# Order of the products in the split-weight projections: second parts of the weights last

## The chip, the cores and the metric

One core of a Trainium2 chip runs the whole program in one launch. The metric is the device time in microseconds of one execution; smaller is better. The times below are medians of runs on the chip. One further execution was profiled, and all rows come from that one.

## The reference, cut to what matters

Two transformer blocks act on 256 tokens of width 1024, all in float32.

```
first_block:   h = modulate(rms_norm(x)), also for 256 context tokens
               p = h @ w_in                       # q, k, v of 8 gated-delta heads and 4 linear-attention heads, gates
               gated delta rule (2 directions) -> @ w_out_a ; gated linear attention (2 directions) -> @ w_out_b
               (gated sum) @ w_out ; x += g1 * y
               mixture of 32 experts, top 4 of 32 ; x += g2 * y ; rms_norm
second_block:  h @ w_in_2 -> dilated attention and latent attention (w_uq_2, w_ukv_2)
               concat(norms) @ w_o_2 ; x += rms_norm(y)
               h @ w_up_2 -> depthwise convolution -> gelu(g) * v -> @ w_down_2 ; x += rms_norm(y)
```

Every `@` outside the experts and the attention cores is a projection of the kind that the change touches.

## The kernel before, in words

**Split weights.** The projections hand TensorE operands of the type `float32r`, and to keep float32's precision each is made of three products. Each float32 operand is split (`split`, lines 48 to 50): ScalarE rounds it to a first part ("hi": tiles `whi`, `hh`, `yT0h`, `hi`), then VectorE subtracts that from the original and leaves the second part ("lo": `wlo`, `hl`, `yT0l`, `lo`). For v of the first two pairs of heads GpSimd does the subtraction. `mm3` (lines 75 to 78) adds hi·hi, hi·lo and lo·hi into one PSUM bank for one block of 128 rows of the contraction. A loop around it goes over the blocks, usually eight.

**Two forms.** Where the output is wanted by feature (`gates`, `gdn_pair`, `stat_proj`, the second block's q and k, its `w_up_2`), the weights are the stationary operand and 256 or 512 tokens move. `mm3`'s second product (line 77) then takes the activations' second part, its third (line 78) the weights'. Where it is wanted by token (`tok_proj`, `out_proj` in `merge`, `tok_mm`, `down`, `down_last`) the activations are stationary and the weights move; there line 77 takes the weights' second part and line 78 the activations'. In the profile's names (out<-moving,stationary) `pj<-hh,wlo` is line 78 of the first form and `pj<-wlo,hh` line 77 of the second.

**Buffers.** The first and the second parts of weights have two buffers each (tags `whi` and `wlo`), each 128 x 1024 elements. ScalarE can round a third piece only when the last product that reads the first piece's `whi` is done; VectorE needs the same of `wlo`. PSUM has two banks for each of the names `pj`, `g` and `sc`.

**Stages, in order of time.** `pre` and `gates`; `gdn` over four pairs of heads, where the projections of the next pair and "fill" work (`lat_act`, `mod_steps`, `gla_proj`) run beside the triangular solve (VectorE, lines 515 and 516, whose result goes through DRAM to the tile `AB`) and the scan of the current pair; `gla` over four heads, each with the projections of the next; `merge` with three output projections, each after `to_feat` has made its activations block by block (transpose on TensorE in line 988, hi on ScalarE in line 990, lo on VectorE in line 991); `moe` with 32 experts whose weights are not split; `post`, the second block.

**What sets the order.** The program text gives priorities. A planner of the tile framework writes each engine's queue at compile time: among the instructions whose operands it reckons to be ready it takes the earliest in the text. Each queue is then worked off in order on the chip, waiting on semaphores. So instructions of different stages stand between each other, transposes among products for instance. The SP queue issues most weight loads, the POOL queue those of `w_in`; a landing buffer `w` is free when both parts were taken from it.

Of the kernel before, what the change touches and what calls it, by code (L numbers as in the profile page):

```python
# [15 lines left out]
P = 128  # L16
# [55 lines left out]
        v.scalar_tensor_tensor(y, a, 1.5, y, op0=OP.add, op1=OP.mult)  # L72


def mm3(nc, out, ah, al, bh, bl, first, last, **kw):
    nc.tensor.matmul(out, ah, bh, start=first, stop=False, **kw)  # L76
    nc.tensor.matmul(out, ah, bl, start=False, stop=False, **kw)  # L77
    nc.tensor.matmul(out, al, bh, start=False, stop=last, **kw)  # L78


def rows_T(K, pool, psum, name, parts):
# [149 lines left out]
def gates(K, dbg=None):  # L231
# [28 lines left out]
    nc.scalar.dma_start(wg[:, :, 32:64], w3[:, :, 7200:7232])  # L260
    wgh, wgl = wsplit(K, wg, P)
    ps = psum.tile([P, 512], F32, name="pj", bufs=2)
    for k in range(8):
        mm3(nc, ps, wgh[:, k, :], wgl[:, k, :], K.hh[:, k, :], K.hl[:, k, :], k == 0, k == 7)
    K.gr = c.tile([64, 512], F32, name="gr")
    nc.scalar.activation(K.gr, ps[:64, :], AF.Copy)

# [123 lines left out]
def gdn_pair(K, pr):  # L391
# [14 lines left out]
    for hh in range(2):  # L406
        h = pr * 2 + hh
        H = Ctx()
        heads.append(H)
        H.h = h  # L410
        H.qT = gp.tile([P, 256], F32, name="qT", bufs=2)
        H.kT = gp.tile([P, 512], F32, name="kT", bufs=4)
        vT = gp.tile([P, 512], F32, name="vT", bufs=1)
        for j, (dst, n) in enumerate(((H.qT, 256), (H.kT, 512), (vT, 512))):

            hi, lo = wsplit(K, ws[hh * 3 + j], P, nc.gpsimd if pr < 2 and j == 2 else None)
            ps = psum.tile([P, 512], F32, name="pj", bufs=2)
            for k in range(8):
                mm3(nc, ps[:, :n], hi[:, k, :], lo[:, k, :], K.hh[:, k, :n], K.hl[:, k, :n], k == 0, k == 7)
            conv_silu(K, ps[:, :n], n, j * 8 + h, dst, nc.vector)  # L420

        pk = K.G()
        for t in range(4):
            nc.tensor.transpose(pk[:, t * P:(t + 1) * P], H.kT[:, t * P:(t + 1) * P], K.ident)
        H.kt = gp.tile([P, 4, P], F32, name="kt", bufs=4)
        nc.scalar.activation(H.kt, pk.rearrange("p (t n) -> p t n", t=4), AF.Copy)
        ns = gp.tile([P, 6], F32, name="ns", bufs=2)
        sq = gp.tile([P, 512], F32, name="th", bufs=2)
        for t in range(4):
            nc.scalar.activation(sq[:, t * P:(t + 1) * P], H.kt[:, t, :], AF.Square, accum_out=ns[:, t:t + 1])  # L430
        pn = K.G()
        sq = gp.tile([P, 512], F32, name="th", bufs=2)
        nc.scalar.activation(sq[:, :2 * P], H.qT, AF.Square)
        for t in range(2):
            nc.tensor.matmul(pn[:, t:t + 1], sq[:, t * P:(t + 1) * P], K.ones[:, 0:1], start=(t == 0), stop=(t == 1),
                             skip_group_check=True)
        nc.vector.tensor_copy(ns[:, 4:6], pn[:, 0:2])
        nq = gp.tile([P, 6], F32, name="nq", bufs=2)
        nc.vector.tensor_scalar(nq, ns, 4 * EPS, None, op0=OP.add)
        r = gp.tile([P, 6], F32, name="r", bufs=2)  # L440
        rsqrt(K, gp, r, nq, 6)

        r2 = gp.tile([P, 6], F32, name="r2", bufs=2)
        nc.vector.tensor_mul(r2, r, r)
        H.d = gp.tile([P, 2, 4], F32, name="d", bufs=4)
        bh = K.beta.rearrange("p d c h -> p d c h")[:, :, :, h]
        nc.vector.tensor_mul(H.d, bh, r2[:, None, 0:4].to_broadcast([P, 2, 4]))
        hn = gp.tile([P, 4], F32, name="hn", bufs=2)
        nc.vector.scalar_tensor_tensor(hn, nq[:, 0:4], 0.5, r[:, 0:4], op0=OP.mult, op1=OP.mult)
        nc.vector.tensor_scalar(K.aq[:, :, h], nq[:, 4:6], 128.0 * EPS, None, op0=OP.mult)  # L450

        pv = K.G()
        for t in range(4):
            nc.tensor.transpose(pv[:, t * P:(t + 1) * P], vT[:, t * P:(t + 1) * P], K.ident)
        H.vs = gp.tile([P, 4, P], F32, name="vs", bufs=4)
        for t in range(4):
            nc.scalar.activation(H.vs[:, t, :], pv[:, t * P:(t + 1) * P], AF.Copy, scale=hn[:, t:t + 1])
        H.dk = gp.tile([P, 2, 4], F32, name="dk", bufs=4)
        nc.vector.tensor_mul(H.dk, H.d, K.kds.rearrange("p (d t h) -> p d t h", d=2, t=4)[:, :, :, h])
# [289 lines left out]
def stat_proj(K, col, n, out):  # L749

    nc = K.nc
    w3 = K.I["w_in"].rearrange("o (k p) n -> p (o k) n", p=P)
    w = K.ring.tile([P, 8, P], F32, name="w")
    nc.gpsimd.dma_start(w, w3[:, :, col:col + P])
    hi, lo = wsplit(K, w, P)
    for k in range(8):
        mm3(nc, out, hi[:, k, :], lo[:, k, :], K.hh[:, k, :n], K.hl[:, k, :n], k == 0, k == 7)


def tok_proj(K, col, tiles, done):  # L760

    nc = K.nc
    w3 = K.I["w_in"].rearrange("o (k p) n -> p (o k) n", p=P)
    ws = []
    for k4 in range(2):
        w = K.ring.tile([P, 4, 256], F32, name="w")
        nc.gpsimd.dma_start(w, w3[:, k4 * 4:k4 * 4 + 4, col:col + 256])
        ws.append(w)
    pss = [K.psum.tile([P, 512], F32, name="pj", bufs=2) for _ in range(len(tiles) // 2)]
    for k4 in range(2):  # L770
        hi = K.wsp.tile([P, 4, 256], F32R, name="whi", bufs=2)
        lo = K.wsp.tile([P, 4, 256], F32R, name="wlo", bufs=2)
        split(K, ws[k4], hi, lo)
        for t in tiles:
            o = pss[t // 2][:, t % 2 * 256:t % 2 * 256 + 256]
            ts = slice(t * P, (t + 1) * P)
            for kk in range(4):
                k = k4 * 4 + kk
                first = k == 0 and t % 2 == 0
                last = k == 7 and t % 2 == 1  # L780
                mm3(nc, o, K.hh[:, k, ts], K.hl[:, k, ts], hi[:, kk, :], lo[:, kk, :], first, last, skip_group_check=True)
    for t in tiles:
        done(t, pss[t // 2][:, t % 2 * 256:t % 2 * 256 + 256])

# [146 lines left out]
def merge(K, rc, dbg=None):  # L931
# [14 lines left out]
    def out_proj(name, lhs_hi, lhs_lo, order, done):  # L946

        pss = {}
        for n, k4 in order:
# [20 lines left out]
            by_token = order is K_OUTER and (n, k4) == order[-1]  # L970
            for t in range(2) if by_token else ():
                done(t, 0, pss[0][t])
            for t, kk in itertools.product(range(2), range(4)) if by_token else ((t, kk) for kk in range(4) for t in range(2)):
                ts, k = slice(t * P, (t + 1) * P), k4 * 4 + kk
                mm3(nc, pss[n][t], lhs_hi[:, k, ts], lhs_lo[:, k, ts], *pairs[kk], k == 0, k == 7)
                if by_token and kk == 3:
                    done(t, n, pss[n][t])
            for t in range(2) if order is N_OUTER and k4 == 1 else ():
                done(t, n, pss[n][t])
# [556 lines left out]
def post(K, dbg=None):  # L1536
# [53 lines left out]
    def tok_mm(name, k_n, col, n, hi, lo, outs):  # L1590

        kk = 2048 // n
        for k0 in range(0, k_n, kk):
            kc = min(kk, k_n - k0)
            w, _ = post_load(K, name, k0, kc, col, n)
            k2 = 0
            while k2 < kc:
                s = min(1024 // n, kc - k2)
                h_, l_ = wpair(1024)
                split(K, w[:, k2 * n:(k2 + s) * n], h_[:, :s * n], l_[:, :s * n])  # L1600
                for i in range(s):
                    k = k0 + k2 + i
                    for t in range(2):
                        ts = slice(t * P, (t + 1) * P)
                        mm3(nc, outs[t], hi[:, k, ts], lo[:, k, ts], h_[:, i * n:(i + 1) * n], l_[:, i * n:(i + 1) * n],
                            k == 0, k == k_n - 1)
                k2 += s


# [70 lines left out]
    for j2 in range(4):  # L1680
        _, wv = post_load(K, "w_in_2", 0, 8, j2 * 256, 256)
        for jj in range(2):
# [2 lines left out]
            hv, lv = (a.rearrange("p (k n) -> p k n", n=P) for a in (h_, l_))  # L1685
            split(K, wv[:, :, jj * P:(jj + 1) * P], hv, lv)
            p = bank("pj")
            for k in range(8):
                mm3(nc, p[:, :256], hv[:, k, :], lv[:, k, :], hi[:, k, :], lo[:, k, :], k == 0, k == 7)
            nc.vector.tensor_mul(qk[:, j, :], p[:, :256], rrb)  # L1690
    va = ap.tile([P, 2, 512], F32, name="va")
    ps = [bank("pj") for _ in range(2)]
# [128 lines left out]
    def down(acc, name, k2, lhs_hi, lhs_lo):  # L1821

        pairs = down_w(name, k2, [wpair(1024) for _ in range(2)])
        for kk, t in ((0, 0), (0, 1), (1, 0), (1, 1)):
            h_, l_ = pairs[kk]
            ts = slice(t * P, (t + 1) * P)
            for n in range(2):
                ns = slice(n * 512, (n + 1) * 512)
                mm3(nc, acc[t][n], lhs_hi[:, kk, ts], lhs_lo[:, kk, ts], h_[:, ns], l_[:, ns], k2 + kk == 0, False)

    def down_last(acc, name, k2, lhs, pairs):

        pairs = down_w(name, k2, pairs[:2]) + down_w(name, k2 + 1, pairs[2:])
        for t in range(2):
            ts = slice(t * P, (t + 1) * P)
            for n in range(2):
                ns = slice(n * 512, (n + 1) * 512)
                for k, (h_, l_) in enumerate(pairs):
                    mm3(nc, acc[t][n], lhs[k][0][:, ts], lhs[k][1][:, ts], h_[:, ns], l_[:, ns], False, k == 3)

    def gained(acc, g, t):

# [62 lines left out]
    for c2 in range(11):  # L1905
        us = {}
        for gv in range(2):
# [3 lines left out]
            for cc in range(2):  # L1911
# [2 lines left out]
                hv, lv = (a.rearrange("p (k n) -> p k n", n=P) for a in (h_, l_))  # L1914
                split(K, wv[:, :, cc * P:(cc + 1) * P], hv, lv)
                p = bank(("pj", "g")[cc])
                for k in range(8):
                    mm3(nc, p[:, :256], hv[:, k, :], lv[:, k, :], hi[:, k, :], lo[:, k, :], k == 0, k == 7)
                u = fp.tile([P, 256], F32, name="u", bufs=8)
                nc.scalar.activation(u, p[:, :256], AF.Identity, scale=K.tap2[1][ct], bias=K.cb2[:, ct:ct + 1])  # L1920
                nc.vector.scalar_tensor_tensor(u[:, 1:], p[:, 0:255], K.tap2[0][ct], u[:, 1:], op0=OP.mult, op1=OP.add)
# [90 lines left out]
```

## Time and profile before

| | |
|---|---|
| median of 3 runs | 2082.15 us (2078.74 to 2091.74) |
| the profiled execution, its own time | 2083.65 us |
| its span, first to last instruction | 2081.9 us |
| mean granted TensorE clock | 0.954 of full speed |
| TensorE matmul / weight load busy | 91% / 56% of the span |
| VectorE / ScalarE / GpSimd busy | 46% / 31% / 9% |
| HBM | 273 GB/s over the span |

Matmul records overlap, since they are pipelined and their ends are modelled, so the busy share is no share of peak. "idle before <-releaser" is the time for which an engine stood before an instruction, and the work whose end let it go on. Start times are microseconds from the span's start.

### The profile page before, as it was taken

To read this page: it belongs to the slowest core of one execution; us is meant where nothing else is said; L and a number is where in the kernel's file an instruction comes from. 1 tells how busy PE (TensorE), PEld (TensorE's weight loads), DVE (VectorE), ACT (ScalarE), POOL (GpSimd) and SP (SyncE) were. 2 spreads that over 40 slices of the span, in tenths; PEclk is the share of its full clock that TensorE was granted. 3 is DMA by queue.
4 is the path that set the end of the run, shared out by engine and by line. 5 is a ranking of instruction groups with operands and counts; after the bars stand their busy time and mean duration, and the time that the engine had idled before them with its cause. 6 is when DMAs were issued, how large, how long until landed. Compare 5 with 4: busy or idle time off the path is not lost. (4 is left out here: it accounts for less than half of the span.)

```text
span 2081.9 us, 27700 instructions
## 1 busy us (share of the span) xinstructions
PE 1898.8 (91%) x10742; PEld 1159.6 (56%) x10743; DVE 965.6 (46%) x2245; ACT 652.5 (31%) x1369; POOL 184.0 (9%) x247
## 2 busy tenths in 40 slices
PE   4796989799998999999999999999999889989998
PEld 1664768687986763333333333333333228779997
DVE  2797785857464641212122221221211137676777
ACT  2553545467554420000000000000000004555554
POOL 1343122211112000000000000000000000000000
PEclk8798999899999989999999999999999988998999
DMA  7347654437544689999999999999999994433551
GB/s 261 77 122 206 183 169 116 112 103 206 169 151 151 254 325 417 417 414 418 417 416 418 418 416 417 418 416 417 418 418 416 417 345 139 140 102 121 183 182 41
DMA packets 191939, 569.60 MB, mean 274 GB/s; under 512 B 47919, under 2 KB 90776, under 8 KB 158650
## 3 DMA queue, kind: packets, MB, share of 16 engines
q1 hardware_dynamic: 160064, 507.19, 63.1%
q0 software_dynamic: 13392, 47.72, 7.4%
q10 hardware_dynamic: 18346, 12.86, 2.5%
q8 instruction: 86, 1.41, 0.3%
q14 instruction: 51, 0.42, 0.1%
HBM read 555.22 MB, written 12.50 MB: 273 GB/s over the span
## 5 line engine op out<-in xcount | busy, mean ns | idle before, releaser
L50 DVE TENSOR_TENSOR wlo<-w,whi 128x1024 fp32r<-128x1024 f32 (+1 forms) x185 | 223.9, 1211 | 132.6 <-ACT whi L49 129.8
L1308 PE MATMUL pg<-w,xT 128*64 128x512 f32 x1024 | 274.4, 605 | 3.5 <-DMA w<-in_w_gu_dram 3.4
L1308 PE MATMUL pl<-w,xT 128*64 128x512 f32 x1024 | 268.1, 593 | 0.0
L49 ACT ACTIVATE whi<-w 128x1024 fp32r<-128x1024 f32 (+1 forms) x189 | 197.3, 1047 | 217.8 <-PE pj L77 70.4
L1330 PE MATMUL po<-w,aT 128*64 128x512 f32 x1024 | 239.9, 608 | 7.1 <-DMA w<-in_w_down_dram 5.7
L1230 ACT ACTIVATE th<-ga 128x512 f32<-128x512 f32 x32 | 20.2, 632 | 613.8 <-DVE ga L1228 613.8
L1338 DVE TENSOR_TENSOR o<-po,g 64x512 f32<-64x512 f32 x64 | 44.1, 689 | 260.1 <-PE po L1330 259.4
L1308 PEld LDWEIGHTS pl<-w,xT 128*64 128x64 f32 x1024 | 75.2, 137 | 146.4 <-issue 146.4
L1330 PEld LDWEIGHTS po<-w,aT 128*64 128x64 f32 x1024 | 69.5, 139 | 141.7 <-issue 121.9
L1308 PEld LDWEIGHTS pg<-w,xT 128*64 128x64 f32 x1024 | 65.2, 136 | 139.4 <-issue 115.9
L1228 DVE TENSOR_SCALAR ga<-pg 128x512 f32<-128x512 f32 x32 | 22.1, 691 | 244.8 <-PE pg L1308 244.8
L77 PE MATMUL pj<-wlo,hh 128*128 128x256 f32 x384 | 116.2, 303 | 2.8 <-DVE wlo L50 2.8
L76 PE MATMUL pj<-whi,hh 128*128 128x256 f32 x384 | 115.2, 300 | 2.9 <-ACT whi L49 2.9
L78 PE MATMUL pj<-whi,hl 128*128 128x256 f32 x384 | 114.6, 299 | 0.0
L76 PE MATMUL pj<-hh,whi 128*128 128x512 f32 (+1 forms) x264 | 100.9, 384 | 12.6 <-ACT hh L49 9.1
L372 DVE SCALAR_TENSOR_TENSOR acc<-padl,taps,acc 128x256 f32<-128x256 f32 x192 | 104.3, 557 | 10.1 <-ACT acc L365 8.0
L78 PE MATMUL pj<-hh,wlo 128*128 128x512 f32 (+1 forms) x264 | 100.0, 380 | 5.9 <-DVE wlo L50 5.7
L77 PE MATMUL pj<-hl,whi 128*128 128x512 f32 (+1 forms) x264 | 100.9, 382 | 0.1
L1288 POOL CAST se<-sel 128x128 fp32r<-128x128 f32 x32 | 22.4, 702 | 828.4 <-PE pl L1292 828.4
L1267 PEld LDWEIGHTS tr<-S,h 128*128 128x128 f32 x480 | 57.9, 191 | 48.6 <-issue 34.9
L77 PEld LDWEIGHTS pj<-wlo,hh 128*128 128x128 f32 x384 | 78.0, 203 | 11.0 <-DVE wlo L50 4.2
L1360 PE MATMUL y<-o,PwT 128*128 128x512 f32 (+1 forms) x136 | 72.2, 641 | 13.0 <-DVE o L1338 10.2
(682 smaller groups left out, 3601.7 us busy)
## 6 DMA issues: line engine op xcount, KB each, us to landing
w<-in_w_gu_dram SPq DMA_DIRECT2D x256, 1024.0 KB, 18.2
w<-in_w_down_dram SPq DMA_DIRECT2D x139, 1024.0 KB, 20.0
w<-in_w_in_dram POOLq DMA_DIRECT2D x72, 512.0 KB, 5.4
w<-in_w_mod_dram SPq DMA_DIRECT2D x48, 512.0 KB, 6.9
w<-in_w_up_dram SPq DMA_DIRECT2D x22, 1024.0 KB, 5.1
w<-in_w_in_dram SPq DMA_DIRECT2D x8, 1024.0 KB, 9.8
gbc<-gD ACTq DMA_DIRECT2D x16, 256.0 KB, 6.2
actD<-la ACTq DMA_DIRECT2D x16, 256.0 KB, 5.0
```

Source lines behind the costliest of these rows:

```text
L49: K.nc.scalar.activation(hi, src, AF.Copy)
L50: (lo_eng or K.nc.vector).tensor_sub(lo, src, hi)
L76: nc.tensor.matmul(out, ah, bh, start=first, stop=False, **kw)
L77: nc.tensor.matmul(out, ah, bl, start=False, stop=False, **kw)
L78: nc.tensor.matmul(out, al, bh, start=False, stop=last, **kw)
L372: eng.scalar_tensor_tensor(al, pl[:, dy:dy + 4, dx:dx + 64], w, al, op0=OP.mult, op1=OP.add)
L1267: nc.tensor.matmul(p[:, kk * P:kk * P + m * CAP], h2[:, t, k * P:(k + 1) * P], S[:, t, e0:e1].rearrange("p e c -> p (e c)"), start=(kk == ...
L1288: nc.gpsimd.tensor_copy(se, sel[:, e, :, None].to_broadcast([P, 2, CAP]))
L1308: nc.tensor.matmul(pp[hs, :], xT[:, k, :], w[:, off + half * 512:off + half * 512 + 512], start=False, stop=(k == 7), skip_group_check=True)
L1330: nc.tensor.matmul(po[dh * CAP:(dh + 1) * CAP, :], aT[:, k % 4, (k // 4) * CAP:(k // 4 + 1) * CAP], w[:, kk * 1024 + dh * 512:kk * 1024 + ...
L1338: nc.vector.tensor_mul(outs[e // 2][e % 2 * CAP:(e % 2 + 1) * CAP, dh * 512:(dh + 1) * 512], po[hs], K.g2[hs])
L1360: nc.tensor.matmul(ps[dh], PwT[g][hs, t, :], outs[g][hs, dh * 512:(dh + 1) * 512], start=(g > 0), stop=True)
```

## The change

`mm3` takes lists of pairs (first part, second part) of the weights (`ws`) and of the activations (`xs`) instead of one block. It first issues, block by block, the products with the weights' first part (hi·hi, then that with the activations' second part), and after all of them the products with the weights' second part. `part` picks one of the two groups; `moving` says that the weights are the moving operand. Callers that write two or four banks from one piece of weights put the group outside the loop over banks. In `out_proj` the group runs over two blocks at a time (its last piece, which goes by token, over four), in `tok_mm` over what one piece of 1024 elements holds, in `down` over one block, in `tok_proj` over four, in `down_last` over four, elsewhere over eight. The numbers of products, splits and transfers stay.

```diff
-def mm3(nc, out, ah, al, bh, bl, first, last, **kw):
-    nc.tensor.matmul(out, ah, bh, start=first, stop=False, **kw)
-    nc.tensor.matmul(out, ah, bl, start=False, stop=False, **kw)
-    nc.tensor.matmul(out, al, bh, start=False, stop=last, **kw)
+def mm3(nc, out, ws, xs, first, last, moving=False, part=(0, 1), **kw):
+    for p in part:
+        for j, ((wh, wl), (xh, xl)) in enumerate(zip(ws, xs)):
+            for i, (w, x) in enumerate(((wl, xh),) if p else ((wh, xh), (wh, xl))):
+                a, b = (x, w) if moving else (w, x)
+                nc.tensor.matmul(out, a, b, start=first and (p, j, i) == (0, 0, 0), stop=last and p == 1 and j == len(ws) - 1,
+                                 **kw)
+def parts(h, l, ks, cs=slice(None)):
+    return [(h[:, k, cs], l[:, k, cs]) for k in ks]
...
 # gates, gdn_pair, stat_proj, q and k and w_up_2 of the second block, alike:
-    for k in range(8):
-        mm3(nc, out, hi[:, k, :], lo[:, k, :], K.hh[:, k, :n], K.hl[:, k, :n], k == 0, k == 7)
+    mm3(nc, out, parts(hi, lo, range(8)), parts(K.hh, K.hl, range(8), slice(n)), True, True)
...
 # tok_proj
-        for t in tiles:
-            for kk in range(4):
-                mm3(nc, o, K.hh[:, k, ts], K.hl[:, k, ts], hi[:, kk, :], lo[:, kk, :], first, last, skip_group_check=True)
+        for p, t in itertools.product(range(2), tiles):
+            mm3(nc, pss[t // 2][:, t % 2 * 256:t % 2 * 256 + 256], parts(hi, lo, range(4)),
+                parts(K.hh, K.hl, range(k4 * 4, k4 * 4 + 4), slice(t * P, (t + 1) * P)), k4 == 0 and t % 2 == 0,
+                k4 == 1 and t % 2 == 1, True, (p,), skip_group_check=True)
...
 # out_proj
+            steps = [(t, range(4), (0, 1)) for t in range(2)] if by_token else \
+                [(t, range(k2 * 2, k2 * 2 + 2), (p,)) for k2 in range(2) for p in range(2) for t in range(2)]
...
 # tok_mm
+                for p, t in itertools.product(range(2), range(2)):
+                    mm3(nc, outs[t], ws, parts(hi, lo, range(k0 + k2, k0 + k2 + s), slice(t * P, (t + 1) * P)), k0 + k2 == 0,
+                        k0 + k2 + s == k_n, True, (p,))
...
 # down
+        for kk, p, t, n in itertools.product(range(2), range(2), range(2), range(2)):
```

## Rows read from the trace of the kernel before

**Rows 1.** The page's busy time, share and count of each engine.
```profile
PE 1898.8 (91%) x10742; PEld 1159.6 (56%) x10743; DVE 965.6 (46%) x2245; ACT 652.5 (31%) x1369; POOL 184.0 (9%) x247
```

**Rows 2.** Busy us (count) per engine in five stretches, then clock, DMA share, GB/s.
```profile
50.00:650.00 600.00, 528.31 (x3980) 438.64 (x3981) 425.77 (x1137) 336.35 (x808) 138.04 (x170) 0.91 0.50 141
650.00:750.00 100.00, 92.00 (x437) 72.79 (x437) 64.38 (x132) 40.73 (x68) 12.34 (x25) 0.96 0.75 278
750.00:1690.00 940.00, 892.27 (x3977) 328.04 (x3979) 193.28 (x334) 64.49 (x115) 21.36 (x29) 0.99 1.01 413
1690.00:1890.00 200.00, 179.46 (x981) 142.59 (x976) 130.39 (x356) 94.23 (x198) 4.86 (x8) 0.90 0.41 138
1890.00:2070.00 180.00, 179.00 (x1262) 168.13 (x1261) 132.31 (x198) 103.00 (x155) 0.00 (x0) 1.00 0.44 147
```

**Rows 3.** PE's waits over the span: who for whom, total us, times, longest.
```profile
PE pj L78 <- DVE wlo L50: 6.7, 3, 5.7
...
PE pj L76 <- ACT whi L49: 3.9, 3, 1.7
...
PE pj L77 <- DVE wlo L50: 3.2, 4, 1.7
```

**Rows 4.** PE's timeline, last two stages: start, us, instruction [idle before <-releaser].
```profile
1816.73 0.51 PE L77 MATMUL pj<-wlo,ch 128*128 128x512 f32 x1 [0.38 <-DVE wlo L50]
...
1896.63 0.39 PE L78 MATMUL pj<-hi,wlo 128*128 128x256 f32 x1 [0.30 <-DVE wlo L50]
...
2039.38 0.38 PE L78 MATMUL pj<-hi,wlo 128*128 128x256 f32 x1 [0.70 <-DVE wlo L50]
2039.60 0.28 PE L76 MATMUL pj<-hi,whi 128*128 128x256 f32 x1
2039.72 0.28 PE L77 MATMUL pj<-lo,whi 128*128 128x256 f32 x1
2039.84 0.28 PE L78 MATMUL pj<-hi,wlo 128*128 128x256 f32 x1
```

**Rows 5.** PE's timeline in the early stretch.
```profile
378.98 0.79 PE L78 MATMUL pj<-hh,wlo 128*128 128x512 f32 x1 [5.67 <-DVE wlo L50]
...
398.31 1.08 PE L424 MATMUL g<-ident,kT 128*128 128x128 f32 x4 [3.90 <-DVE kT L378]
...
483.79 0.39 PE L77 MATMUL pj<-wlo,hh 128*128 128x256 f32 x1 [1.66 <-DVE wlo L50]
...
502.56 0.66 PE L556 MATMUL sc<-AB,mt 32*32 32x32 f32 x9 [0.55 <-DMA AB<-solD]
```

**Rows 6.** ScalarE's timeline behind the wait at 378.98.
```profile
385.31 1.19 ACT L457 ACTIVATE vs<-g,hn 128x128 f32<-128x128 f32 x4 [5.14 <-DVE hn L449]
...
387.33 0.39 ACT L364 ACTIVATE padl<-pj 128x256 f32<-128x256 f32 x1
```

**Rows 7.** ScalarE's timeline in the second feed-forward, two splits.
```profile
1919.32 1.06 ACT L49 ACTIVATE whi<-w 128x1024 fp32r<-128x1024 f32 x1 [1.37 <-PE g L77]
...
1922.20 1.06 ACT L49 ACTIVATE whi<-w 128x1024 fp32r<-128x1024 f32 x1 [1.06 <-PE pj L77]
```

**Rows 8.** ScalarE's timeline in the second block's first projection.
```profile
1726.30 1.06 ACT L49 ACTIVATE whi<-w 128x1024 fp32r<-128x1024 f32 x1 [0.32 <-PE pj L78]
```

**Rows 9.** PE's timeline at the start of the first output projection.
```profile
660.00 1.12 PE L988 MATMUL g<-ident,rows 128*128 128x128 f32 x4 [3.17 <-DVE yT0l L991]
660.77 0.78 PE L77 MATMUL pj<-wlo,yT0h 128*128 128x512 f32 x1
661.34 0.63 PE L78 MATMUL pj<-whi,yT0l 128*128 128x512 f32 x1
661.77 0.47 PE L988 MATMUL g<-ident,rows 128*128 128x128 f32 x1
```

**Rows 10.** Busy us per engine as in rows 2, in two short stretches.
```profile
373.00:383.00 10.00, 4.33 (x13) 3.23 (x12) 9.11 (x27) 1.14 (x3) 3.79 (x4) 0.51 0.37 100
...
397.00:404.00 7.00, 5.69 (x27) 5.72 (x28) 5.86 (x9) 3.62 (x8) 3.87 (x4) 0.51 0.88 176
```

More of the change, by code (lines that the diff above doesn't have):

```diff
@@ L262, in gates @@
     ps = psum.tile([P, 512], F32, name="pj", bufs=2)
-    for k in range(8):
-        mm3(nc, ps, wgh[:, k, :], wgl[:, k, :], K.hh[:, k, :], K.hl[:, k, :], k == 0, k == 7)
+    mm3(nc, ps, parts(wgh, wgl, range(8)), parts(K.hh, K.hl, range(8)), True, True)
     K.gr = c.tile([64, 512], F32, name="gr")
@@ L417, in gdn_pair @@
             ps = psum.tile([P, 512], F32, name="pj", bufs=2)
-            for k in range(8):
-                mm3(nc, ps[:, :n], hi[:, k, :], lo[:, k, :], K.hh[:, k, :n], K.hl[:, k, :n], k == 0, k == 7)
+            mm3(nc, ps[:, :n], parts(hi, lo, range(8)), parts(K.hh, K.hl, range(8), slice(n)), True, True)
             conv_silu(K, ps[:, :n], n, j * 8 + h, dst, nc.vector)
@@ L755, in stat_proj @@
     hi, lo = wsplit(K, w, P)
-    for k in range(8):
-        mm3(nc, out, hi[:, k, :], lo[:, k, :], K.hh[:, k, :n], K.hl[:, k, :n], k == 0, k == 7)
+    mm3(nc, out, parts(hi, lo, range(8)), parts(K.hh, K.hl, range(8), slice(n)), True, True)
 def tok_proj(K, col, tiles, done):
@@ L773, in tok_proj @@
         split(K, ws[k4], hi, lo)
-        for t in tiles:
-            o = pss[t // 2][:, t % 2 * 256:t % 2 * 256 + 256]
-            ts = slice(t * P, (t + 1) * P)
-            for kk in range(4):
-                k = k4 * 4 + kk
-                first = k == 0 and t % 2 == 0
-                last = k == 7 and t % 2 == 1
-                mm3(nc, o, K.hh[:, k, ts], K.hl[:, k, ts], hi[:, kk, :], lo[:, kk, :], first, last, skip_group_check=True)
+        for p, t in itertools.product(range(2), tiles):
+            mm3(nc, pss[t // 2][:, t % 2 * 256:t % 2 * 256 + 256], parts(hi, lo, range(4)),
+                parts(K.hh, K.hl, range(k4 * 4, k4 * 4 + 4), slice(t * P, (t + 1) * P)), k4 == 0 and t % 2 == 0,
+                k4 == 1 and t % 2 == 1, True, (p,), skip_group_check=True)
     for t in tiles:
@@ L972, in out_proj @@
                 done(t, 0, pss[0][t])
[L973 to L976, printed above, removed]
+            steps = [(t, range(4), (0, 1)) for t in range(2)] if by_token else \
+                [(t, range(k2 * 2, k2 * 2 + 2), (p,)) for k2 in range(2) for p in range(2) for t in range(2)]
+            for t, kks, p in steps:
+                mm3(nc, pss[n][t], [pairs[kk] for kk in kks],
+                    parts(lhs_hi, lhs_lo, [k4 * 4 + kk for kk in kks], slice(t * P, (t + 1) * P)), k4 == 0 and kks[0] == 0,
+                    k4 == 1 and kks[-1] == 3, True, p)
+                if by_token:
                     done(t, n, pss[n][t])
@@ L1600, in tok_mm @@
                 split(K, w[:, k2 * n:(k2 + s) * n], h_[:, :s * n], l_[:, :s * n])
[L1601 to L1606, printed above, removed]
+                ws = [(h_[:, i * n:(i + 1) * n], l_[:, i * n:(i + 1) * n]) for i in range(s)]
+                for p, t in itertools.product(range(2), range(2)):
+                    mm3(nc, outs[t], ws, parts(hi, lo, range(k0 + k2, k0 + k2 + s), slice(t * P, (t + 1) * P)), k0 + k2 == 0,
+                        k0 + k2 + s == k_n, True, (p,))
                 k2 += s
@@ L1687, in post @@
             p = bank("pj")
-            for k in range(8):
-                mm3(nc, p[:, :256], hv[:, k, :], lv[:, k, :], hi[:, k, :], lo[:, k, :], k == 0, k == 7)
+            mm3(nc, p[:, :256], parts(hv, lv, range(8)), parts(hi, lo, range(8)), True, True)
             nc.vector.tensor_mul(qk[:, j, :], p[:, :256], rrb)
@@ L1823, in down @@
         pairs = down_w(name, k2, [wpair(1024) for _ in range(2)])
-        for kk, t in ((0, 0), (0, 1), (1, 0), (1, 1)):
+        for kk, p, t, n in itertools.product(range(2), range(2), range(2), range(2)):
             h_, l_ = pairs[kk]
[L1826 to L1829, printed above, removed]
+            ns = slice(n * 512, (n + 1) * 512)
+            mm3(nc, acc[t][n], [(h_[:, ns], l_[:, ns])], parts(lhs_hi, lhs_lo, (kk,), slice(t * P, (t + 1) * P)), k2 + kk == 0,
+                False, True, (p,))
     def down_last(acc, name, k2, lhs, pairs):
@@ L1837, in down_last @@
                 ns = slice(n * 512, (n + 1) * 512)
-                for k, (h_, l_) in enumerate(pairs):
-                    mm3(nc, acc[t][n], lhs[k][0][:, ts], lhs[k][1][:, ts], h_[:, ns], l_[:, ns], False, k == 3)
+                mm3(nc, acc[t][n], [(h_[:, ns], l_[:, ns]) for h_, l_ in pairs], [(h_[:, ts], l_[:, ts]) for h_, l_ in lhs],
+                    False, True, True)
     def gained(acc, g, t):
@@ L1916, in post @@
                 p = bank(("pj", "g")[cc])
-                for k in range(8):
-                    mm3(nc, p[:, :256], hv[:, k, :], lv[:, k, :], hi[:, k, :], lo[:, k, :], k == 0, k == 7)
+                mm3(nc, p[:, :256], parts(hv, lv, range(8)), parts(hi, lo, range(8)), True, True)
                 u = fp.tile([P, 256], F32, name="u", bufs=8)
```

## The prediction, made before the changed kernel was run

> **What bounds the kernel now.** I began with the busy shares of the whole span. TensorE (PE) is busy for 1898.8 us of 2081.9, VectorE (DVE) for less than half of it [rows 1]. An average over unlike stages says little, so the second view was the busy time by stage [rows 2]. Five stretches are to be seen. From 50 to 650 us (the gated-delta and linear-attention stages) PE is busy 528 of 600 us at a granted clock of 0.91, with 426 us of DVE beside it. From 650 to 750 us (three output projections, routing) it is 92 of 100. From 750 to 1690 us the experts run: the DMA engines are full (share 1.01, 413 GB/s), and the change touches nothing there. From 1690 to 1890 us the second block's attention has PE at 179 of 200 at a clock of 0.90. From 1890 to 2070 us the second feed-forward has PE at 179.0 of 180 at full clock: that stretch is PE's own work, and no reordering of it gains more than the missing microsecond.
>
> The third view was what PE waited for [rows 3]. Waits for a second part ("wlo", made by VectorE in line 50) in front of a product with two parts come to 6.7 us in 3 waits (line 78) and 3.2 us in 4 (line 77): 9.9 us, 0.5% of the span. Waits for a first part ("whi") come to 3.9 us. That is the whole visible stock the change can draw on. The fourth view was the order of time around each of these waits, to see what ends last there; that decides the sum.
>
> **The change, part by part.** It removes and adds no product, no split and no transfer. In each projection it moves the products with a weight's second part behind all those with its first part; for weights that move (token-major forms) it also brings the product with the activations' second part up from third place to second. SP's, ACT's and POOL's queues issue the same DMAs, and a weight's landing buffer comes free after the second-part subtraction, as now.
>
> *A product that no longer waits for "wlo".* Before: with 512 columns, one product with the first part runs, then PE stands until VectorE is done. After: all first-part products run meanwhile, 16 of 24 where one split holds eight k-blocks. The seven waits are of two kinds.
> - In the last two stages three are to be seen: 0.38, 0.30 and 0.70 us [rows 4]. PE is the engine that ends those stretches, so their 1.4 us should come off. Late next is nothing that the profile shows within a split's 1.2 us.
> - The early ones make up the other 8.5 us; the largest are 5.67 and 1.66 [rows 5]. I take their gain as nothing. Behind the 5.67 us wait the product's reader is ScalarE, and its queue is held by the scaling of "vs" until 385.3 us for a VectorE result (5.14 us idle), then by a split; it copies the product out at 387.33 [rows 6]. PE would finish sooner and the copy would start no earlier. PE itself then waits 3.90 us for "kT" at 398.31, which VectorE ends; this wait would grow by what was won. Behind the 1.66 us wait PE comes to 502.56 and still waits 0.55 us for the solved triangles to come back by DMA: again the winner waits longer at the next door. Bounds: 0, and all of it, 8.5 us.
>
> *The first part's buffer comes free after two thirds of a projection.* ScalarE often waits for that buffer. In the feed-forward its splits follow each other every 2.88 us after waits of 1.37 and 1.06 us on PE [rows 7]. That is PE's own pace, so ScalarE being earlier is worth nothing there. In the attention's first projection, at 1726.30, the split had waited 0.32 us [rows 8], so no more than that was held up by the buffer. Bounds 0 to the 3.9 us of PE's waits for "whi" [rows 3]; I take 0, as PE's pace or ScalarE's own queue ends them.
>
> *The activations' second part is wanted one place earlier* in the moving-weight form. Where a projection starts while its activations are still being made (three output projections, and the first of the second block) the second product now needs what VectorE writes last. At the first of these PE waited 3.17 us for that tile at a transpose, and the product with "wlo" at 660.77 ran ahead of the one with "yT0l" at 661.34 [rows 9]. This filler goes to the end of its group. Per start the bounds are 0 (the planner has transposes to put there, as it does now) and 3.2 us; nearest is what the other order leaves between the two products now, 0.57 us less the 0.43 a product takes at the lower clock, about 0.15 [rows 9]. Four starts: 0.6 us, with 0 to 12.7 as ends.
>
> *Spacing of products.* In the feed-forward the second of three products shares its stationary operand with the first and the third doesn't, yet each begins 0.12 us after the one before, at 256 columns [rows 4]. I cost the new sequence of loads at nothing, for the PE row gives no cheaper step to lose.
>
> **The sum.** The profiled execution took 2083.65 us, 1.75 around its span of 2081.9. Minus 1.4, plus 0.6, gives 2082.9. It stood 1.5 us above the median of the three runs (2082.15, from 2078.74 to 2091.74), so the median I expect is 2081 us. A change under 1% (21 us) can't be told from none here.
>
> **The rivals.**
>
> *All visible waits are won.* 9.9 us of "wlo" and 3.9 of "whi" come off, and with the stop at 373 the lower clock that followed: the granted clock was 0.51 from 373 to 383 [rows 10]. PE was busy for 4.3 us in the first, which at full clock is 2.2. Together 16 us, 2067 us. For it: PE is the busiest engine in every stage concerned. Against: the doors at 387, 398 and 502 us. Chance 0.18. The Trainium skill, page "TensorE: Matmul & The Clock Gate", section "Why this matters for your kernels", advises against idle gaps between bursts of matmuls because the clock falls after them. The low clock beginning where PE stood agrees with it; by that rule alone a closed gap would pay this case's 2.2 us on top, but from 397 to 404 us the clock is 0.51 too [rows 10], behind the "kT" wait that the change makes longer, so the same rule can take it back.
>
> *Slower: the wait passes from the weights' second part to the activations'.* Place: the four starts above. Price: if PE stands at the second product with transposes queued behind it, the transposes that would make the next activations stand as well, and each start loses up to the 3.17 us of the row; four make 12.7 us, without the 1.4 won: 2096 us. It decides as soon as "yT0l" of a k-block comes later than one product, 0.43 us, after "yT0h"; VectorE's two-part loop there is slower than that, since PE waited 3.17 us for it [rows 9]. Against it: queues are ordered by readiness at compile time, and transposes already stand between products in those rows. Chance 0.16.
>
> *The planner makes another program.* It orders each queue by its own estimate of when operands are ready; with products ready earlier it may interleave the early stages otherwise, so that the change isn't just the one written down. The room is PE's idle time: 71.7 us from 50 to 650 us and 8 from 650 to 750 [rows 2]. A third of it, 27 us, either way would be 2054 or 2108. No row speaks for a sign. Chance 0.10, half each way.
>
> The Trainium skill, page "Perfetto Trace Analysis", section "Identifying the Most-Contended Engine", would judge PE by its weight loads rather than by matmul occupancy. The rows put these at 168 of 180 us in the feed-forward and at 439 of 600 in the early stretch [rows 2]. By that rule the early stretch has room where occupancy shows little, and a better order could win there, which is the planner's faster half; the waits behind "kT" and the solve agree that PE isn't the only bound there.
>
> **How the numbers follow.** Forecast 0.56, all waits won 0.18, passed-on wait 0.16, another program 0.10. The likeliest gives 2081; its own range is 2073 (the early 8.5 won) to 2086. The range of 8 in 10 takes in the first two rivals with a few microseconds of spread between runs: 2064 to 2098; what is left out is mainly the planner's. Faster by over 1% (under 2061): half of the planner's case and a part of the first rival's, 0.10. Slower by over 1% (over 2103): the other half and the upper end of the passed-on wait, 0.07. Within 1%: 0.83.
>
> **What would show it.** Right: waits of PE for "wlo" nearly gone, the waits for "kT" and for the solve's DMA longer by some microseconds, the feed-forward stretch the same within 2 us, and the start of the experts within 3 us of now. Wrong: if the experts start 8 us or more earlier, the doors were no doors; if "yT0l" or "lo" stands before products in the projections' starts, the wait was passed on; if transposes and scan products stand elsewhere among the projections of the early stretch, the planner did more than was written.

## The result, and the profile after

The changed kernel takes 2111.37 us (median of 4 runs, 2109.9 to 2113.14), the one before 2080.44 us on the same chip: ratio 1.0127, 95% interval 1.0096 to 1.0157. It is slower by 1.3%, outside the predicted range of 2064 to 2098.

The page of the changed kernel, busy time and count of each engine; beside [rows 1] the counts are the same but for four on ScalarE (ACT), which loads its function tables 10 times instead of 14, and TensorE's (PE's) busy time has grown by 11 us:

```profile
PE 1910.1 (90%) x10742; PEld 1170.1 (55%) x10743; DVE 975.7 (46%) x2245; ACT 651.2 (31%) x1365; POOL 184.7 (9%) x247
```

The five stretches of [rows 2], with edges moved by what the stages are late (columns as there):

```profile
50.00:685.00 635.00, 545.20 (x3981) 451.55 (x3982) 434.68 (x1133) 334.79 (x804) 137.31 (x169) 0.89 0.46 133
685.00:785.00 100.00, 93.12 (x437) 73.75 (x435) 64.50 (x135) 40.49 (x67) 12.66 (x25) 0.93 0.76 284
785.00:1725.00 940.00, 890.90 (x3985) 327.24 (x3987) 192.79 (x332) 64.34 (x115) 21.35 (x29) 0.99 1.01 413
1725.00:1920.00 195.00, 174.68 (x960) 139.05 (x957) 129.80 (x355) 93.48 (x198) 4.87 (x8) 0.90 0.42 141
1920.00:2100.00 180.00, 180.00 (x1274) 169.47 (x1273) 132.80 (x198) 103.65 (x155) 0.00 (x0) 1.00 0.44 147
```

All of the loss is in the first row. The first output projection's transposes start at 686.8 us instead of 652.2 and the first expert's products at 794.5 instead of 759.9: 34.6 us late at both, so nothing is lost between them. From there to the end it takes 1317.0 us instead of 1322.0.

Some of what PE waited for over the whole span, after (who for whom: us, times, longest):

```profile
PE sc L564 <- DMA AB<-solD: 8.4, 2, 5.9
PE g L443 <- ACT th L441: 8.0, 2, 4.6
PE pj L82 <- DVE la L694: 7.0, 1, 7.0
PE pj L82 <- ACT whi L49: 6.5, 4, 2.2
PE sc L574 <- ACT x L568: 6.3, 3, 3.9
PE pj L82 <- ACT acc L374: 5.9, 3, 4.6
PE pj L82 <- DVE wlo L50: 3.8, 1, 3.8
```

Four of these before (lines 76, 435 and 556 of that kernel are lines 82, 443 and 564 of this one):

```profile
PE g L435 <- ACT th L433: 6.5, 3, 2.5
PE sc L556 <- DMA AB<-solD: 5.0, 4, 3.5
PE pj L76 <- ACT acc L365: 2.2, 3, 1.2
PE pj L76 <- DVE la L686: 1.2, 1, 1.2
```

The waits for "wlo" have shrunk from 9.9 us [rows 3] to 3.8 in one (5.67 was the largest [rows 5]), as the products' order lets expect. Others have grown, those for "x" are new, and they stand before other kinds of instructions: products of the triangular solve (`sc`), norms (`g L443`), first products of a projection whose bank ACT or VectorE (DVE) has not emptied. Not all grew: the waits for "kT" fell from 10.2 to 8.7 us.

The queues are others. Comparing the two traces queue by queue up to the first output projection, by tile names and shapes (for PE with the first and second part of an operand taken as one), at most 668 of ACT's 832 instructions, 926 of DVE's 1201 and 3543 of PE's 4092 stand in the same order among each other in both kernels. (The expectations below count instructions of the built programs, 899 for ACT and 1366 for DVE.) The planner wrote another program. One place of it, PE and then ACT:

```profile
411.40 0.28 PE L82 MATMUL pj<-whi,hl 128*128 128x256 f32 x1
416.28 1.02 PE L443 MATMUL g<-ones,th 128*128 128x1 f32 x4 [4.60 <-ACT th L441]
417.15 1.09 PE L462 MATMUL g<-ident,vT 128*128 128x128 f32 x4
417.90 0.56 PE L82 MATMUL pj<-wlo,hh 128*128 128x256 f32 x1
```

```profile
406.65 0.61 ACT L434 ACTIVATE kt<-g 128x512 f32<-128x512 f32 x1
414.12 0.63 ACT L386 ACTIVATE th<-acc 128x512 f32<-128x512 f32 x1 [3.55 <-DVE acc L381]
414.66 0.29 ACT L438 ACTIVATE th<-kt 128x128 f32<-128x128 f32 x1
415.82 0.40 ACT L441 ACTIVATE th<-qT 128x256 f32<-128x256 f32 x1
```

The squares of "kt" had their input from 407.3 us on. They stand behind a tanh that waits for DVE, so ACT idles 3.55 us before it gets to them. PE idles 4.60 us for the last square (of "qT"), with the "wlo" products of a projection behind it in its queue; DVE's last subtraction before them had ended at 407.4. The operands are there; the order of two queues keeps the engines from them.

### The profile page after: what moved, and what is told of

Same layout as the page of the kernel before. It is cut to its first block, busy times and chain, and to the rows that moved or that the text cites. A ratio compares the mean times of both kernels' runs of the same rounds, so it can differ in the third digit from the quotient of the medians.

```text
span 2111.5 us, 27732 instructions
## 1 busy us (share of the span) xinstructions
PE 1910.1 (90%) x10742; PEld 1170.1 (55%) x10743; DVE 975.7 (46%) x2245; ACT 651.2 (31%) x1365; POOL 184.7 (9%) x247
## 5 line engine op out<-in xcount | busy, mean ns | idle before, releaser
L82 PE MATMUL pj<-whi,hh 128*128 128x256 f32 x384 | 102.2, 300 | 9.0 <-ACT whi L49 6.5
L82 PE MATMUL pj<-whi,hl 128*128 128x256 f32 x384 | 100.1, 295 | 0.0
L82 PEld LDWEIGHTS pj<-whi,hh 128*128 128x128 f32 x384 | 77.7, 202 | 13.3 <-ACT whi L49 9.2
L1367 PE MATMUL y<-o,PwT 128*128 128x512 f32 (+1 forms) x136 | 71.3, 633 | 14.1 <-DVE o L1345 10.2
L1230 DVE TENSOR_TENSOR x<-x,y 128x512 f32<-128x512 f32 x68 | 46.5, 686 | 76.8 <-PE y L1367 76.8
L82 PEld LDWEIGHTS pj<-whi,hl 128*128 128x128 f32 x384 | 77.7, 202 | 0.2
```

Of the source, the lines that this page charges most:

```text
L82: nc.tensor.matmul(out, a, b, start=first and (p, j, i) == (0, 0, 0), stop=last and p == 1 and j == len(ws) - 1, **kw)
L1230: nc.vector.tensor_add(y[:, t, ds_], y[:, t, ds_], p)
L1367: nc.tensor.matmul(ps[dh], PwT[g][hs, t, :], outs[g][hs, dh * 512:(dh + 1) * 512], start=(g > 0), stop=True)
```

## The experiments

Theories: **P**, the loss comes from the new order that the planner gave all the other instructions; **D**, the new order of the products costs by itself. Ratios are against the kernel before on the same chip; some 20 us are 1%. No kernel leaves out any work. Further theories (R, S, A, W, N) are told in the expectations of the runs that they belong to. Code is shortened.

**early_old**: the old products in the early stages (`mm3o` is `mm3` as it was before), the new from `merge` on.

```diff
 # gates, gdn_pair, stat_proj, tok_proj
-    mm3(nc, out, parts(hi, lo, range(8)), parts(K.hh, K.hl, range(8), slice(n)), True, True)
+    for k in range(8):
+        mm3o(nc, out, hi[:, k, :], lo[:, k, :], K.hh[:, k, :n], K.hl[:, k, :n], k == 0, k == 7)
...
```

> The new order from merge on, the old order of products in gates, gdn_pair, stat_proj and tok_proj. Theory P (the planner: the 31 us come from another order of the other instructions in the queues) and theory D (direct: the new order of the products itself holds banks and first parts longer) both expect the stretch before merge as in the kernel before, and the some 5 us that the changed kernel's milestones win back after 750 us kept: 2075 (2068 to 2082). If it stays above 2095, the loss is made after the early stretch and both are wrong.

Measured: 2083.69 us, ratio 0.9996 (0.9971 to 1.0020), above the 2068 to 2082 expected. The loss is made by the early stages. The 5 us of the later stages did not show: by this interval those are worth something between 6 us won and 4 lost. All sixteen profiles with the new order from `merge` on have the stretch from the experts to the end 2 to 6 us shorter than the one profile of before; that alone doesn't prove a gain.

**pin_new**: the changed kernel, every queue tied to the order of before up to the end of `gla` (an edge of issue order from each instruction to the one before it).

```diff
         gla(K)
+        # in short; ORDER: one list per queue, as built for the kernel before
+        for names in ORDER:
+            for a, b in zip(names, names[1:]):
+                tc.add_manual_dep(here[b], a, NoSync)
```

> The changed kernel, with every queue's order up to the end of gla pinned to the order that the queues of the kernel before have; each projection's products stand in the same places, in the new order. Theory P: the loss is gone, and what the early wlo waits (8.5 us) are worth shows against the run with old products in the early stages: 0 to 8 us below it, 2066 to 2078. Theory D: the products' order costs by itself, so near the changed kernel, 2100 to 2112.

Measured: 2085.40 us, ratio 1.0006 (0.9980 to 1.0033). In the queues of before, the new order of the products costs nothing that shows (at most 7 us by the interval), against D. It also wins nothing that shows; P's 2066 to 2078 was too low by what the later stages and the early waits were thought to be worth. The pins held: compared as above, the early queues of pin_new differ from those of before in no more than two places each. The trace shows where the waits went. The waits of PE between 368 and 398 us, first early_old (old products, the same queues):

```profile
368.35 0.61 PE L451 MATMUL g<-ones,th 128*128 128x1 f32 x4 [2.22 <-ACT th L449]
375.12 0.80 PE L89 MATMUL pj<-hh,wlo 128*128 128x512 f32 x1 [5.36 <-DVE wlo L50]
394.12 1.08 PE L440 MATMUL g<-ident,kT 128*128 128x128 f32 x4 [3.81 <-DVE kT L394]
```

and pin_new:

```profile
371.41 0.61 PE L443 MATMUL g<-ones,th 128*128 128x1 f32 x4 [2.22 <-ACT th L441]
378.20 2.11 PE L82 MATMUL pj<-hh,wlo 128*128 128x512 f32 x8 [0.89 <-DVE wlo L50]
387.66 0.39 PE L82 MATMUL pj<-whi,hh 128*128 128x256 f32 x1 [2.37 <-ACT padc L376]
393.10 0.39 PE L82 MATMUL pj<-whi,hh 128*128 128x256 f32 x1 [2.07 <-ACT whi L49]
397.36 1.09 PE L432 MATMUL g<-ident,kT 128*128 128x128 f32 x4 [3.88 <-DVE kT L387]
```

The wait for "wlo" falls from 5.36 to 0.89 us. PE then waits 2.37 us for a bank that ACT has not emptied and 2.07 for a rounding. From the norms to the "kT" transposes it is 25.8 us in the one and 26.0 in the other.

**tok_old** and **gdn_old**: the changed kernel with one caller in the old order.

> The changed kernel with tok_proj alone in the old order. Theory D, in the form that tok_proj's four tiles finish late and hold both pj banks: 2080. Theory P: this is one more order of the queues, and nothing forecasts its time; between 2060 and 2110, with no reason that the loss be undone.

> The changed kernel with gdn_pair's q, k and v alone in the old order. Theory D, in the form that the q, k, v projections leave their banks and weights later: 2080. In the form of tok_proj: 2111. Theory P: another order of the queues, between 2060 and 2110.

Measured: 2103.19 us, ratio 1.0094 (1.0068 to 1.0120), and 2099.61 us, ratio 1.0060 (1.0036 to 1.0084). Neither form of D gives its 2080. Each is one more order of the queues, and each is slow.

**one05, one0, one02**: 24 products of one projection permuted, of some 4000.

```diff
 # early_old, gdn_pair
+    if pr == 0 and hh * 3 + j == 5:      # one0: 0, one02: 2
+        mm3(nc, ps[:, :n], parts(hi, lo, range(8)), parts(K.hh, K.hl, range(8), slice(n)), True, True)
+    else:
         for k in range(8):
             mm3o(...)
```

> The kernel before, but the last of pair 0's six projections in gdn_pair (24 products of some 4000 on TensorE in the early stretch) in the new order. The planner then writes other queues: of ScalarE's 899 early instructions 690 keep their order. Theory R (the loss is that of any other order of the queues; the one of before happens to be a good one): slower though next to nothing was changed, 2090 to 2112. Theory S (the new product order misleads the planner in each projection, and the losses add up): a 24th of the loss, 2082 to 2086.

> The same with the first of pair 0's projections instead: 821 of ScalarE's 899 and 1160 of VectorE's 1366 early instructions keep the order of before. Theory R: slower, or by luck equal, 2083 to 2105, and not the same as one05. Theory S: 2082 to 2086.

> The kernel before with the third of pair 0's projections in the new order and nothing else: 715 of ScalarE's 899 early instructions keep the order of before. One more order of the queues that has no reason to be better or worse. Theory R (the one of before is a good one among many): slower, 2088 to 2112. If orders scatter evenly about that of before, as likely faster: 2060 to 2085.

The expectations call these, and g2 below, the kernel before; from `merge` on they have the new order as early_old has, whose ratio was 0.9996. Measured: one05 2110.27 us, ratio 1.0115 (1.0071 to 1.0158); one0 2092.07, 1.0033 (1.0009 to 1.0057); one02 2095.02, 1.0052 (1.0030 to 1.0075). Permuting 24 products costs up to nine tenths of the whole loss, depending on which 24. A loss that adds up over projections would have given a 24th.

**old_in_one05**: early_old's products, all old, with the queues pinned to the order built for one05.

> The products of early_old (all of them in the old order up to the end of gla), with every queue up to there pinned to the order that the planner wrote for one05. No product differs from early_old, whose time was that of before; only the queues do. Order of the queues as the cause: 2104 to 2114, like one05. The permuted 24 products as the cause: 2080 to 2090.

Measured: 2113.09 us, ratio 1.0134 (1.0104 to 1.0164). No early product differs from early_old, the early queues in the trace are those of one05, and the loss is there. With pin_new this shows P from both sides: old products in other queues lose as much as one05 does, new products in the queues of before lose nothing that shows. The first of these is shown for one05's queues, not for the changed kernel's own.

**one05_act**: one05 with ACT's queue pinned to the order of before.

> one05 (24 products of one projection permuted, 25 us slower) with ScalarE's queue pinned to the order of before; the planner's other queues then come back near to that of before by themselves (3534 of 3663 early instructions of TensorE, 1278 of 1366 of VectorE). The order of the queues as the only cause: the 25 us are gone, 2080 to 2090. The permuted products as a cause of their own: 2100 to 2112.

Measured: 2084.16 us, ratio 0.9985 (0.9962 to 1.0008). The 25 us are gone.

**g2**: second parts last in `gdn_pair` in groups of two blocks.

> The kernel before with gdn_pair's second parts last in groups of two blocks instead of eight; the whi buffers are then released and wlo asked for almost as before. Theory S (the misleading grows with how far the products move): 2083 to 2088. Theory R: one more order of the queues (729 of ScalarE's 899 keep theirs), 2088 to 2112.

Measured: 2082.22 us, ratio 0.9995 (0.9975 to 1.0015): no loss, 0.8 us under S's range and well under R's, for which it would be a draw that came out even. ACT keeps 729 of 899 instructions in order here and 821 in one0, which loses 7 us, so how much is reordered does not tell the time.

**pin_pe, pin_act, free_act**: the changed kernel with only PE's, only ACT's, or all queues but ACT's pinned.

> The changed kernel with TensorE's queue alone pinned, up to the end of gla, to the order of before; the planner orders ScalarE's, VectorE's, GpSimd's and SP's queues by itself. If the loss lies in where scan products, transposes and projections stand on TensorE: 2083 (2076 to 2090). If it lies in ScalarE's queue, where roundings stand ahead of the copies that the scan waits for: 2098 to 2112.

> The same with ScalarE's queue alone pinned. If the loss lies in ScalarE's queue: 2083 (2076 to 2090). If in TensorE's: 2098 to 2112.

> The changed kernel with the queues of TensorE, VectorE, GpSimd and SP pinned, up to the end of gla, to the order of before, and ScalarE's left to the planner (768 of its 899 early instructions keep the order of before). Theory A (ScalarE's order carries the loss, since pinning it alone took the loss away): 2094 to 2112. If no one queue carries it and an order is bad by how the queues fit each other, this one, near the order of before in all queues: 2080 to 2092.

Measured: 2094.70 us, 1.0034 (1.0012 to 1.0056); 2089.67, 1.0008 (0.9981 to 1.0035); 2091.85, 1.0037 (1.0017 to 1.0058). Holding ACT's order takes the loss away, but holding PE's or the other four takes most of it away too. pin_pe lies between what its two theories expected; free_act misses A's range and lies at the upper end of the other, 2080 to 2092. No single queue carries the loss.

**new_in_g2, new_in_one02**: the new products (but those of `tok_proj` in `gla_proj`) in the pinned queues of g2 and one02.

> The queues of g2, pinned up to the end of gla, with the new order of products in all stages (gla_proj's four-tile tok_proj keeps the old one). g2 took the time of before although TensorE waits 26.9 us for wlo in its early stretch, the longest 12.5 us; these waits go. Theory W (with the queues held, a removed wait pays where it is large): 2060 to 2070. Theory N (the next wait in the queue takes it over, as in pin_new, where 8.2 us of such waits went and nothing was won): 2078 to 2088.

> The same products in the pinned queues of one02, which was some 10 us slower than before and waits 17.8 us for wlo there. Theory W: 2078 to 2084. Theory N: 2090 to 2098.

Measured: 2093.13 us, ratio 1.0033 (1.0008 to 1.0058), and 2090.32, ratio 1.0042 (1.0025 to 1.0059). Some of PE's waits before `merge`, g2 first, then new_in_g2:

```profile
PE pj L82 <- DVE wlo L50: 12.7, 2, 12.5
PE pj L88 <- DVE wlo L50: 11.5, 5, 4.3
PE pj L82 <- DVE la L702: 4.5, 1, 4.5
PE g L451 <- ACT th L449: 4.4, 3, 2.2
PE sc L572 <- DMA AB<-solD: 4.2, 3, 2.2
PE pj L89 <- DVE wlo L50: 2.8, 1, 2.8
```

```profile
PE pj L82 <- DVE wlo L50: 11.3, 4, 9.8
PE sc L570 <- DMA AB<-solD: 9.6, 3, 3.5
PE g L449 <- ACT th L447: 9.5, 5, 3.4
PE pj L82 <- DVE la L700: 8.1, 1, 8.1
```

Of 27 us of waits for "wlo" some 16 go, and the solve's DMA, the norms and a bank held by DVE take 14 more than in g2. The one02 pair differs by 0.1%, inside the intervals. W is out, and what N says is seen in three orders: a removed wait is handed on. In g2's queues it seems to be handed on at a loss, 0.4% above g2 itself (on another chip, and the two intervals overlap a little), which N did not expect: PE's busy time before `merge` is 10 us longer (526 and 536, one profile each) with the granted clock at 0.91 instead of 0.93. So the new products may cost something in queues made for other products. What they cost in the changed kernel's own queues is open: no run puts the old products into those.

## Why the prediction was wrong

**Where the 34.6 us are.** From 50 us to the first output projection, in this order: before, after, early_old, pin_new, one05, old_in_one05 (columns as in [rows 2]; the second number is the length).

```profile
50.00:652.20 602.20, 530.51 (x3992) 439.99 (x3993) 426.54 (x1139) 337.05 (x810) 138.33 (x171) 0.91 0.50 140
```

```profile
50.00:686.80 636.80, 547.00 (x3991) 452.53 (x3991) 435.41 (x1135) 335.18 (x805) 137.60 (x170) 0.89 0.46 133
```

```profile
50.00:648.00 598.00, 525.14 (x3988) 434.71 (x3987) 423.03 (x1127) 333.31 (x803) 134.69 (x169) 0.92 0.49 140
```

```profile
50.00:652.40 602.40, 527.09 (x3992) 435.44 (x3993) 425.70 (x1135) 336.77 (x809) 133.75 (x170) 0.92 0.50 140
```

```profile
50.00:680.80 630.80, 540.84 (x3992) 449.35 (x3993) 429.71 (x1143) 338.87 (x811) 137.40 (x171) 0.89 0.48 134
```

```profile
50.00:688.90 638.90, 542.33 (x3992) 451.04 (x3992) 429.15 (x1139) 338.74 (x810) 137.42 (x171) 0.88 0.47 132
```

Length less PE's busy time is its idle time: 71.7 us before, 89.8 after, 72.9 and 75.3 in early_old and pin_new, 90.0 and 96.6 in the two with one05's queues. So 18.1 of the 34.6 us are more idling, in many waits of 1 to 7 us. The other 16.5 are the same number of matmuls being busy for longer. In the six rows PE is busy for 525 to 531 us at a granted clock of 0.91 or 0.92, and for 541 to 547 at 0.88 or 0.89. The clock is not all of it: pin_act and one02 both stand at 0.91 in this stretch, with 536.9 and 530.9 us busy. How much of the 16.5 us the clock makes is not separated.

**The step that failed** is that the sum took the places of all other instructions as given. A re-planning of the queues stood in it at nothing; it had a place only as the third rival, "The planner makes another program", with a chance of 0.10, half each way, since "No row speaks for a sign". It was worth 31 us, and pin_new takes them away by holding the queues. The rival's mechanism was what happened; that its price of 27 us is near is luck, for it was a third of PE's idle time, and only 18.1 of the 34.6 us are idle time. The runs say more on the sign. Seven orders that the planner wrote for the early stretch other than that of before (the changed kernel, tok_old, gdn_old, one05, one0, one02, g2) stand at -0.05% to +1.27%, mean +0.68%, none faster beyond the noise. The order of before is a good one of those that the planner may write, and the changes tried here that made it write another lost or came out even. All seven have some early products in the new order, so it is open whether an unrelated edit would lose as much, or whether this order of products leads the planner astray. That the order of before was kept for being good is my reading; what makes it good is not settled, beyond that PE idles less before the first output projection (71.7 us, against 75.7 to 92.6 in the seven) and is granted a higher clock than in the four slowest (0.91 against 0.89).

**The steps that held, once the queues are held.** *Early waits worth nothing*: pin_new is 1.0006. The doors were partly others than named: the wait for "kT" did not grow (3.81 and 3.88 us), a bank and a rounding took 4.4 us in front of it; the solve's DMA took more, as forecast (5.1 us of PE's early waits in early_old, 8.9 in pin_new). *The buffer of the first part, worth 0*: true of the time, though the buffer moved much. ACT's waits in front of its 73 early roundings, in early_old, pin_new and the changed kernel (busy us, mean ns | idle before, releasers):

```profile
L49 ACT ACTIVATE whi<-w 128x1024 fp32r<-128x1024 f32 x73 | 76.8, 1057 | 47.9 <-PE pj L88 25.1 <-PE pj L89 11.6 <-issue 7.8
```

```profile
L49 ACT ACTIVATE whi<-w 128x1024 fp32r<-128x1024 f32 x73 | 76.8, 1056 | 30.5 <-PE pj L82 28.7 <-DVE rs_a L71 1.6
```

```profile
L49 ACT ACTIVATE whi<-w 128x1024 fp32r<-128x1024 f32 x73 | 77.0, 1057 | 96.2 <-PE pj L82 60.5 <-issue 13.9 <-DMA w<-in_w_in_dram 12.4
```

With the queues held the buffer does come free sooner and ACT waits 17 us less; in the planner's own order for the changed kernel it waits twice as long.

*The last two stages, -1.4 us*: no wait for "wlo" is left there, PE is busy for 180 of 180 us in the feed-forward, the roundings still follow each other every 2.88 us as in [rows 7], and a gain of that size can't be told in early_old. *Spacing of products, 0*: in the changed kernel, too, products of 256 columns begin 0.12 us after each other (406.72 and 406.84 us). *The slower rival*, the wait passed to the activations' second part, did not happen. At the first output projection PE stands as in [rows 9]:

```profile
694.67 1.12 PE L995 MATMUL g<-ident,rows 128*128 128x128 f32 x4 [3.21 <-DVE yT0l L998]
695.44 0.78 PE L82 MATMUL pj<-whi,yT0l 128*128 128x512 f32 x1
696.01 0.63 PE L82 MATMUL pj<-whi,yT0h 128*128 128x512 f32 x1
```

3.21 us against 3.17, at a transpose, not at a product; nor does the 0.6 us of the sum show, for the experts are as late as this stage. *All visible waits won* fell with pin_new. Of the signs named for a wrong prediction the third is the one that came: scan products and norms stand elsewhere among the projections.

The room that the prediction drew from the Trainium skill, page "Perfetto Trace Analysis", section "Identifying the Most-Contended Engine", for the planner's faster half was not found: weight loads fill 73% of the early stretch before (440 of 602 us) and 71% after (453 of 637), and none of the seven orders was faster.

## What to carry to other kernels

Where a planner writes the queues, compare the queues as built before reasoning about an edit: here 24 permuted products left 690 of ScalarE's 899 instructions in order and cost 25 us. Price an edit with the queues pinned, and the re-planning by itself; if the present order is the best of those seen, expect the re-planning to lose. In the three pinned orders here a stall at one instruction was no stock to be won: find the next instruction that is late with the first one removed.

## What the runs showed of the hardware that was not expected

TensorE's granted clock in the changed kernel, four stretches around the first pair's solve and scan (columns as in [rows 2]):

```profile
201.00:204.00 3.00, 0.66 (x6) 0.46 (x4) 0.00 (x0) 0.00 (x0) 2.43 (x3) 0.92 0.62 198
204.00:213.00 9.00, 4.29 (x20) 4.29 (x21) 4.77 (x8) 3.13 (x5) 3.12 (x4) 0.50 1.02 287
232.00:248.00 16.00, 15.14 (x161) 10.51 (x160) 10.10 (x17) 5.57 (x11) 2.54 (x3) 1.00 0.75 189
248.00:268.00 20.00, 19.07 (x169) 11.71 (x167) 7.99 (x24) 7.41 (x13) 0.00 (x0) 0.50 0.31 112
```

The first fall, to 0.50 (1.2 of 2.4 GHz), comes in a wait of 7.05 us. The Trainium skill, page "TensorE: Matmul & The Clock Gate", section "Why this matters for your kernels", expects that of idle gaps, and the row agrees. The kernel before has a fall like it, at 0.51 from 192 to 206 us with PE busy for 8.0 of the 14. The second fall does not follow an idle stretch: PE had been busy for 15.1 of 16 us, and it is busy for 19.1 of the 20 us at half clock. In the kernel before, the solve's and scan's small products of this stretch ran between 243 and 262 us at full clock with PE busy for 17.1 of 19. From 160 us to the end of pair 0's scan (283 us before, 292 after) PE idles for 19.7 us before and 19.3 after; it is busy for 103.3 and 112.8 us, at a mean clock of 0.92 and 0.84, so pair 0 ends 9 us later without idling more. What brought the clock down is not shown; it was not tried.
